# Matrix product with leaky ReLU by two levels of Strassen-Winograd: three more products in quarters, paired output transfers, and kept sums of B

## The chip, the cores and the metric

The kernel runs on one core of one Trainium2 chip. The core has five engines with queues of their own: PE (matmul), DVE (VectorE), ACT (ScalarE), POOL (GpSimd) and SP (SyncE, which here only issues DMAs). The metric is the device time of one execution in microseconds (us), as the median of several runs.

## The reference

```python
def setup_inputs():
    m, k, n = 4096, 4096, 4096
    return {"a": np.random.randn(m, k).astype(np.float32),
            "b": np.random.randn(k, n).astype(np.float32), "alpha": np.float32(0.01)}

def reference(a, b, alpha):
    x = np.matmul(a, b)
    return np.where(x > 0, x, alpha * x)
```

## The kernel before

A and B are rounded to 16-bit floats on the way in; the sums are kept in 32 bits. The output is cut into 4 groups of 1024 rows (g = 0 to 3) and 4 pairs of 1024 columns (j = 0 to 3). One such block (g, j) is a *region*; the first of all is done in the plain way, the other 15 stand in the list `regions` and are done one behind the other: j = 1, 2, 3 for g = 0, then 2, 0, 3, 1 for groups 1 and 2, and 2, 0, 1, 3 for group 3. Groups 2 and 3 are thus (2,2), (2,0), (2,3), (2,1), (3,2), (3,0), (3,1), (3,3).

**First level.** In a region A is a 2 x 2 of blocks a11 to a22, and B of b11 to b22 (a block is 512 x 2048 or 2048 x 512, in two halves k of 1024 along the inner dimension). Winograd's scheme needs seven products instead of eight, in the order of `PRODUCTS`: a11 b11, a12 b21, s2 T2, s3 T3, s1 T1, a22 T4, s4 b22. Here s1 to s4 are sums of blocks of A, made once in a group, and T1 to T4 are sums of blocks of B, made by DVE in place: T3 = b22 - b12 over b12, T2 = b11 + T3 over b11, and so on (`b_sum`, line 603). A whole product is 64 matmuls of 128 x 128 by 512 columns in the function `product` (line 831). It goes into four banks of PSUM, each 128 rows x 512 columns ("row tile" mt = 0 to 3). The eight banks are two sets, y and z, that change places with each region. After the first product ACT copies y to z (line 1132), so that the second product can be added on z while the third is added on y.

**Second level.** A product can be done in quarters: its operands are cut again into 2 x 2, and seven *quarter products* of 16 matmuls of 256 columns (`quarter_product`, line 770) take the place of eight. That needs four sums of the operand of A and four of that of B, of 128 x 2048 numbers each (`sums_of_a`, `sums_of_b`, lines 696 to 719 and 753; those of s1, s4, a22 are made once in a group, kept in DRAM and loaded as needed), and some copies and adds between banks. Before the change, groups 1 to 3 do the products of s3, s1, a22 and s4 in quarters; in most regions the order on PE is first, second, third product whole, then s1, s3, a22, s4 in quarters (`fifth_in_quarters`, `fourth_by_seeds`, `sixth_in_quarters`, `seventh_in_quarters`). The last region of a group ("turning") does most products whole, because ACT, DVE and POOL bring in the next group's A there.

**Order.** The order on each engine is written out by hand: every engine's queue holds its instructions in the order of the program. A buffer that is taken from a pool waits for the release of an earlier tile there. The 128 x 2048 buffers (`new_a16`, three of them), the tile `t` of four such (pool `x`) and the `c` tiles (32-bit results on their way out) matter here.

**Around the edge of two regions.** The seventh product of a region writes y, a bank `one` and a bank `other`; ACT copies (lines 999, 1003, 1008) and DVE adds (1005, 1009 from `other`, 1011 from y) collect it in the `c` tiles `kept_c`; then `leave` does the leaky ReLU on DVE (line 313) and SP issues the output (line 1076, one DMA for each row tile).

**Start of a region.** After the first product come the copies y to z, then T3 and T2 (line 603) out of b11, b12, b22. For j = 2, T3 and T2 are written to DRAM in group 1 and loaded in groups 2 and 3 in their place (`move_t`, line 529; T2 on ACT's queue, T3 as a part of `fetch_unit`). s2 is loaded in two halves (line 789), the second behind a DVE memset (line 788).

**Measures.** The kernel checks that the magnitudes of rows of A and columns of B are alike. For each block a *measure* squares four parts of 128 x 2048 on ACT (line 231) and adds them on DVE (lines 240 to 264). `EARLY` and `MEASURED` say in which region which block is measured: those of `EARLY` around the first product, the "middle" one of `MEASURED` around T3 and T2. At the end the last region decides from all (`judge`, lines 635 to 651), and a plain bf16 product would replace the result if they weren't alike.

Of the kernel before, what the change touches and what calls it, by code (L numbers as in the profile page):

```python
# [24 lines left out]
KC = 8  # L25
# [12 lines left out]
OTHERS = (0, 3)  # L38

# [9 lines left out]
def kernel(  # L49
# [464 lines left out]
    kept_t = {name: dram_pool.tile([2, P, KC * NT], DT, name=f"kept_{name}") for name in ("t3", "t2")}  # L514
# [12 lines left out]
    def move_t(name, t, k, out, queue=nc.sync):  # L527
        ends = kept_t[name][k], t.rearrange("p c n -> p (c n)")
        queue.dma_start(*(ends if out else ends[::-1]))

    def fetch_unit(i, u, nt, later=False):
# [7 lines left out]
        if g > 1 and j == CACHED and (half, nt) == (0, 1):  # L539
            move_t("t3", t, u, False)  # L540
# [89 lines left out]
    def judge(line):  # L630
# [29 lines left out]
        (1, 3): [B11], (2, 0): [B21], (2, 3): [B21], (2, 1): [B12], (3, 1): [B11, B21],  # L660
# [15 lines left out]
    FIFTH = {(1, 0), (1, 3), (2, 0), (2, 3), (3, 0), (3, 1), (3, 3)}  # L676
# [123 lines left out]
    in_quarters = False  # L800
    for i, (g, j) in enumerate(regions):
# [6 lines left out]
        ybank = 0 if i % 2 == 0 else 4  # L808
        zbank = 4 - ybank
# [6 lines left out]
        def product(n, banks, first):  # L816
            name, half, nt = PRODUCTS[n]

# [3 lines left out]
            if n == 0 or n == 2 and in_fourth:  # L822
                order[-16:] = [(mt, k, c) for mt in range(MT) for k, c in todo[-4:]]
            elif n == 1 or n == 4 and in_fourth:
                order[:16] = [(mt, k, c) for mt in range(MT) for k, c in todo[:4]]
# [14 lines left out]

        def keep(banks, side):
            pairs, kept = new_c(side)
            for mt in range(MT):
                nc.scalar.copy(kept[mt], banks[mt])  # L844
            return pairs, kept

# [51 lines left out]
        def fifth_in_quarters(y, banks, tq, sx, pairs, between):  # L898
# [6 lines left out]
            onto = lambda r, n: [y[2 * r + m][:, n * HALF:(n + 1) * HALF] for m in range(2)]  # L905
# [6 lines left out]
            def more(r, n, room):  # L912
                for m, to in enumerate(onto(r, n)):
                    nc.vector.tensor_add(to, to, room[:, m])

            quarter_product(x[0, 1], b[1, 0], onto(0, 0))
            quarter_product(x[0, 0], b[0, 0], into(chain), True)
            one = copied(0, 0, chain)
            quarter_product(a_quarter(sx[4]), b[1, 1], onto(0, 1))
# [3 lines left out]
            quarter_product(x[1, 1], t(4), onto(1, 0))  # L923
# [9 lines left out]
            last = copied(1, 1, chain)  # L933
            for m in range(2):
# [3 lines left out]
        def sixth_in_quarters(pairs, banks, v_pairs, v, y, tq, sq):  # L938
# [20 lines left out]
            add(v, y)  # L959
# [28 lines left out]
        def seventh_in_quarters(y, one, other, tq, sq):  # L988
# [7 lines left out]
            onto = lambda r, n: [y[2 * r + m][:, n * HALF:(n + 1) * HALF] for m in range(2)]  # L996
            quarter_product(x[0, 1], b[1, 0], onto(0, 0))
# [3 lines left out]
            quarter_product(x[1, 1], t(4), onto(1, 0))  # L1001
# [3 lines left out]
            nc.vector.tensor_add(block(0, 1), pair(other), block(0, 1))  # L1005
            quarter_product(sx(3), b[0, 1], into(one))
            for n in (1, 0):
                nc.scalar.copy(block(1, n), pair(one))
            nc.vector.tensor_add(block(1, 1), pair(other), block(1, 1))
            for mt in range(MT):  # L1010
                nc.vector.tensor_add(kept[mt], y[mt], kept[mt])
            return pairs

        def seventh_at_the_end(y, one, other, tq, sq, one_more):
# [9 lines left out]
            onto = lambda r, n: [part(y[2 * r + m], n) for m in range(2)]  # L1024
# [8 lines left out]
            for mt in (2, 3):  # L1033
                nc.scalar.copy(part(kept[mt], 1), part(y[mt], 1))
            quarter_product(x[0, 1], b[1, 0], onto(0, 0))
            for mt in range(2):
                more(mt, 0, part(y[mt], 0))
# [7 lines left out]
            quarter_product(sx(4), b[1, 1], onto(0, 1))  # L1045
            for mt in range(2):
                more(mt, 1, part(y[mt], 1))
# [7 lines left out]
            quarter_product(x[1, 1], t(4), onto(1, 0), by_row=True)  # L1055
            for mt in (2, 3):
                more(mt, 0, part(y[mt], 0))
# [12 lines left out]
        def leave(pairs, h, nt, some=(0, 1)):  # L1070
            for r, t in enumerate(pairs):
# [3 lines left out]
                for m in range(2):  # L1075
                    nc.sync.dma_start(place(g, h, 2 * r + m, j, nt), t[:, m, :])  # L1076
# [34 lines left out]
        y = [new_bank(ybank + mt) for mt in range(MT)]  # L1111
        z = [new_bank(zbank + mt) for mt in range(MT)]
# [6 lines left out]
        in_fifth = (g, j) in FIFTH  # L1119
        second_of_group = in_fourth and regions[i - 2][0] != g  # L1120
        early = [measure(i, *block) for block in EARLY.get((g, j), [])]
        for m in early[:1]:
# [3 lines left out]
        product(0, y, True)  # L1126
        if second_of_group:
            sums_of_s3(g, (2,))
        for m in early[:1]:
            m.end()  # L1130
        for mt in range(MT):
            nc.scalar.copy(z[mt], y[mt])  # L1132
        if second_of_group and g in [of for of, _ in FIFTH]:
            sums_of_a(g, "s1", new_a16)
        for m in early[1:]:
            m.begin()
# [19 lines left out]
        for m in early[1:]:  # L1156
# [43 lines left out]
        if in_fifth:  # L1200
# [8 lines left out]
        if in_fifth:  # L1209
# [6 lines left out]
        for k in ks:  # L1216
            halves_of = [slice(None)]
            if in_fifth and k == ks[1]:
# [7 lines left out]
            if in_fourth and k == ks[0]:  # L1226
                y7 = quarters_of_b(i, 0, 1)
                t3_of_b(y7)
                if not in_fifth:
                    tq = {n: new_a16() for n in (2, 1)}  # L1230
                    sums_of_b(y7, tq, (2, 1))
# [8 lines left out]
        z = [new_bank(zbank + mt) for mt in range(MT)]  # L1240
# [234 lines left out]
```

## Time and profile before

| | |
|---|---|
| median of 3 runs | 1524.78 us (1524.66 to 1526.13) |
| profiled execution, its own time | 1526.13 us |
| span from the first to the last instruction | 1524.2 us |
| mean granted clock of TensorE | 0.999 |
| DMA traffic | 372.29 MB, 244 GB/s on average |
| regions (2,0), (2,3), (3,0), (3,1), each from its start to the next region's | 90.34, 90.35, 90.34, 90.35 us |
| regions (1,0), (1,3) | 91.85, 91.90 us |
| turning regions (1,1), (2,1) | 95.11, 95.11 us |

How to read it: times in a row are us from the span's start. A row of the order in time has start, length, engine, line, operation, output and inputs, the count of merged instructions, and in brackets the idle time ahead with what ended it. A PE row's length goes to the modelled end of its last matmul, so rows overlap by some tenths; starts are compared. A row of waits has the waiting engine and line, what it waited for, then total, count and longest. A row of a stretch has its ends, its length, the busy time (and count) of PE, weight loads, DVE, ACT and POOL, then the granted clock, the DMA share and GB/s. "q" behind an engine's name is its queue of DMAs.

### The profile page before, as it was taken

The numbers are of one execution on the slowest core, as the hardware profiler recorded it, in microseconds if no ns is written. First come the engines' busy times: TensorE is split into PE (matmuls) and PEld (weight loads), VectorE is DVE, ScalarE is ACT, GpSimd is POOL, SyncE is SP. The second block draws the span as 40 slices with busy tenths as digits, with TensorE's granted clock in tenths as the row PEclk, the third lists the DMA queues.
The fourth block names the chain that finished last, engine by engine and source line by source line (L and its number), as shares of the span: only waits on it lengthen the run. The fifth ranks groups of instructions, "written<-read, shape, count | busy, mean of one in ns | idle before, by whom it ended". The sixth has DMA issues, their size and how long they took to land.

```text
span 1524.2 us, 22803 instructions
## 1 busy us (share of the span) xinstructions
PE 1512.9 (99%) x9003; PEld 879.2 (58%) x9003; DVE 1166.7 (77%) x1221; ACT 512.2 (34%) x885; POOL 258.3 (17%) x426
## 2 busy tenths in 40 slices
PE   9999999999999999999999999999999999999998
PEld 4444444444446577584544748667554475848667
DVE  4588867666896597777779598777978779888797
ACT  2411535537410123124661132323574113252221
POOL 5641110233202011012320101000331100101000
PEclk9999999999999999999999999999999999999999
DMA  9999995999889999999898968859999894968935
GB/s 247 189 215 206 242 285 164 174 187 193 235 330 247 285 300 288 290 289 271 199 273 317 287 252 187 312 151 330 220 239 313 223 337 148 276 238 205 331 122 172
DMA packets 197767, 372.29 MB, mean 244 GB/s; under 512 B 19345, under 2 KB 132241, under 8 KB 184594
## 3 DMA queue, kind: packets, MB, share of 16 engines
q0 software_dynamic: 119808, 112.22, 46.7%
q1 hardware_dynamic: 71218, 232.95, 41.0%
q10 hardware_dynamic: 6624, 25.56, 4.3%
q8 instruction: 72, 1.18, 0.3%
q14 instruction: 45, 0.37, 0.1%
HBM read 359.66 MB, written 121.11 MB: 315 GB/s over the span
## 4 chain that ended last, share of the span: by engine, by line
PE 58%; DMA 6%; DVE 1%; issue 1%; SPq 0%; POOL 0%; DVEq 0%; POOLq 0%
PE ps L831 34%; PE ps L770 25%; DMA b<-in_b_dram 5%; DMA q<-kept_qs 1%; DVE b L603 0%; DVE c L313 0%; DVE c L1028 0%; POOL b L547 0%; SPq L1076 0%; DVE b L696 0%; DVE b L1225 0%; SPq L762 0%; DVEq L603 0%; DVEq L313 0%; POOLq L547 0%
## 5 line engine op out<-in xcount | busy, mean ns | idle before, releaser
L831 PE MATMUL ps<-b,a 128*128 128x512 f16 x2624 | 570.6, 379 | 0.0
L831 PEld LDWEIGHTS <-a 128*128 128x128 f16 x2624 | 256.7, 98 | 307.8
L831 PE MATMUL ps<-b,s 128*128 128x512 f16 x1792 | 391.3, 379 | 0.0
L831 PEld LDWEIGHTS <-s 128*128 128x128 f16 x1792 | 175.4, 98 | 210.9
L603 DVE TENSOR_TENSOR b<-b 128x4096 f16<-128x4096 f16 x97 | 218.9, 2286 | 51.3 <-DMA b<-in_b_dram 33.1
L547 POOL DMA_DIRECT2D b<-in_b_dram x128 | 94.8, 745 | 870.5 <-PE ps L770 266.1
L770 PEld LDWEIGHTS <-q 128*128 128x128 f16 x1872 | 182.6, 98 | 23.2 <-DMA q<-kept_qs 1.6
L844 ACT COPY c<-ps 128x512 f32<-128x512 f32 x164 | 85.9, 596 | 287.5 <-PE ps L831 277.7
L133 POOL DMA_DIRECT2D a<-in_a_dram x252 | 137.5, 553 | 246.5 <-ACT junk L622 81.3
L142 DVE STREAM_TRANSPOSE a<-a 128x512 uint32<-128x512 uint32 (+2 forms) x120 | 127.0, 1107 | 66.5 <-DMA a<-in_a_dram 66.5
L313 DVE SCALAR_TENSOR_TENSOR c<-c 128x1024 f32<-128x1024 f32 (+2 forms) x123 | 141.9, 1196 | 17.7 <-ACT c L844 17.4
L622 ACT ACTIVATE junk<-a 128x512 bf16<-128x512 f16 x192 | 121.2, 631 | 72.8 <-DMA a<-in_a_dram 67.7
L770 PEld LDWEIGHTS <-a 128*128 128x128 f16 x1200 | 117.4, 98 | 14.7
L231 ACT ACTIVATE sq<-b 128x2048 bf16<-128x2048 f16 x60 | 111.3, 1911 | 43.1 <-DVE sq L240 36.7
L770 PE MATMUL ps<-b,q 128*128 128x256 f16 x1008 | 118.6, 273 | 0.0
L283 PE MATMUL ps<-b,a 128*128 128x512 f16 x512 | 112.2, 379 | 0.5 <-ACT a L380 0.2
L770 PEld LDWEIGHTS <-s 128*128 128x128 f16 x960 | 93.8, 98 | 14.2 <-DVE b L603 1.3
L770 PE MATMUL ps<-q,q 128*128 128x256 f16 x864 | 99.9, 273 | 0.9 <-DMA q<-kept_qs 0.9
L770 PE MATMUL ps<-b,a 128*128 128x256 f16 x752 | 88.3, 273 | 0.0
L283 PEld LDWEIGHTS <-a 128*128 128x128 f16 x512 | 49.7, 98 | 60.8 <-issue 1.4
L1132 ACT COPY ps<-ps 128x512 f32<-128x512 f32 x60 | 32.8, 572 | 147.8 <-PE ps L831 147.8
L1063 DVE TENSOR_TENSOR c<-ps,c 128x512 f32<-128x512 f32 x72 | 44.6, 683 | 47.6 <-PE ps L831 38.0
(125 smaller groups left out, 1053.6 us busy)
## 6 DMA issues: line engine op xcount, KB each, us to landing
b<-in_b_dram POOLq DMA_DIRECT2D x136, 512.0 KB, 12.4
out_dram<-c SPq DMA_DIRECT2D x240, 256.0 KB, 7.8
a<-in_a_dram POOLq DMA_DIRECT2D x244, 128.0 KB, 5.7
b<-kept_half SPq DMA_DIRECT2D x28, 1024.0 KB, 11.8
b<-kept SPq DMA_DIRECT2D x20, 1024.0 KB, 9.2
q<-kept_qs ACTq DMA_DIRECT2D x40, 512.0 KB, 7.2
s<-kept_s SPq DMA_DIRECT2D x18, 1024.0 KB, 9.1
q<-kept_qs SPq DMA_DIRECT2D x28, 512.0 KB, 6.1
```

The lines of the kernel that those rows point to most:

```text
L133: nc.gpsimd.dma_start(a16[32 * q:32 * q + 32], src.rearrange("(g i) w -> i g w", i=32))
L142: nc.vector.transpose(part.rearrange("p c m e -> p c (m e)").bitcast(U32) .rearrange("p c (g i) -> p g c i", i=32), src[:, :, i * n:(i + 1 ...
L231: nc.scalar.activation(to, self.parts[n], SQUARE)
L283: nc.tensor.matmul(ps, a_cols(at[0, h, u], c, mt, (h, u) == (0, 0)), bt[0, u, nt][:, c, :], start=first, stop=last,)
L313: nc.vector.scalar_tensor_tensor(t, t, alpha, t, op0=MULT, op1=MAX if alpha <= 1 else MIN)
L547: nc.gpsimd.dma_start(t[:, c:c + 4, :], b_rows(j, u, c, 4, nt, g > 0))
L603: nc.vector.tensor_tensor(f(to), f(x0), f(x1), op)
L622: nc.scalar.activation(junk, piece[:, q, :], SQUARE, accum_out=to[:, 4 * n + q:4 * n + q + 1])
L770: nc.tensor.matmul(to[m], xq[:, c // 2, rows, c % 2], yq[:, c, :], start=first and c == 0 and m < banks, stop=c == KC - 1, skip_group_chec ...
L831: nc.tensor.matmul(banks[mt], a_cols(t, c, mt, t is first_a), B(half, nt, k)[:, c, :], start=first and (k, c) == todo[0], stop=(k, c) == t ...
L844: nc.scalar.copy(kept[mt], banks[mt])
L1063: nc.vector.tensor_add(to, bank, to)
```

## The change

1. The first product (a11 b11) of (2,3), (3,1) and (3,3) is done in quarters (`first_in_quarters`). Its sums are made by DVE: seven in steps between the quarter products of the seventh product of the region before (`for_the_first`), the eighth in the first product. The four banks of y then hold quarters instead of row tiles, so the second and third product of these regions are cut into matmuls of 256 columns, and all helpers that read y or z go by quarters there. s2 is loaded behind the first product in these regions.
2. `leave` issues one DMA for two row tiles.
3. T3 and T2 are also kept for j = 0 and 3: written in group 2, loaded in group 3.
4. Measures: B21 of j = 0 goes from (2,0) to (3,0), B11 of j = 1 from (3,1) to (1,1). In a region whose first product is in quarters, or which loads T2, the early measures come behind the copies to z; where T2 is loaded, such a measure is begun and ended at once.
5. The set `FIFTH` (all regions in question had their fifth product in quarters) and the branches for the others go.

```diff
+KEPT_T = {CACHED: 1, 0: 2, 3: 2}
...
+    def places(g, h, mt, j, nt):
+        row = ((g * 2 + h) * MT + mt) * P
+        col = (j * 2 + nt) * NT
+        return out[row:row + 2 * P, col:col + NT].rearrange("(m p) n -> p m n", p=P)
...
-        if g > 1 and j == CACHED and (half, nt) == (0, 1):
-            move_t("t3", t, u, False)
+        if g > KEPT_T.get(j, G) and (half, nt) == (0, 1):
+            move_t("t3", j, t, u, False)
...
     EARLY = {
-        (1, 3): [B11], (2, 0): [B21], (2, 3): [B21], (2, 1): [B12], (3, 1): [B11, B21],
+        (1, 3): [B11], (1, 1): [B11], (2, 3): [B21], (2, 1): [B12], (3, 0): [B21], (3, 1): [B21],
     }
...
+    FIRST = {(2, 3), (3, 1), (3, 3)}
...
+        in_first = (g, j) in FIRST
+        if in_first:
+            shared_bank = Z[1]
+            Y, Z = [Z[2], Z[3], Y[0], Z[0]], [Y[1], Y[2], Z[1], Y[3]]
+        else:
+            Y, Z = Z, Y
...
+            if in_first:
+                for k in ks:
+                    for q in (0, 1, 3, 2):
+                        for c in range(KC):
+                            for m, to in enumerate(into(banks[q])):
+                                nc.tensor.matmul(
+                                    to, a_cols(operand(g, name, k), c, q // 2 * 2 + m),
+                                    B(half, nt, k)[:, c, q % 2 * HALF:(q % 2 + 1) * HALF],
+                                    start=False, stop=(k, c) == (ks[-1], KC - 1), skip_group_check=True,
+                                )
+                return
...
-        def seventh_in_quarters(y, one, other, tq, sq):
+        def seventh_in_quarters(y, one, other, tq, sq, between):
...
+            quarter_product(x[0, 1], b[1, 0], onto(y, 0, 0))
             quarter_product(x[0, 0], b[0, 0], into(one), True)
             nc.scalar.copy(block(0, 0), pair(one))
-            quarter_product(sx(4), b[1, 1], onto(0, 1))
-            quarter_product(x[1, 1], t(4), onto(1, 0))
+            quarter_product(sx(4), b[1, 1], onto(y, 0, 1))
+            next(between)
+            quarter_product(x[1, 1], t(4), onto(y, 1, 0))
+            next(between)
             quarter_product(sx(2), t(2), into(one))
             nc.scalar.copy(block(0, 1), pair(one))
+            next(between)
             quarter_product(sx(1), t(1), into(other), True)
+            next(between)
             nc.vector.tensor_add(block(0, 1), pair(other), block(0, 1))
             quarter_product(sx(3), b[0, 1], into(one))
+            next(between)
             for n in (1, 0):
                 nc.scalar.copy(block(1, n), pair(one))
             nc.vector.tensor_add(block(1, 1), pair(other), block(1, 1))
-            for mt in range(MT):
-                nc.vector.tensor_add(kept[mt], y[mt], kept[mt])
+            add_pieces(pairs, y)
             return pairs
+
+        def for_the_first(tq, sq, first_t, first_s):
+            y1 = quarters_of_b(i + 1, 0, 0)
+            x1 = {key: by_chunk(q) for key, q in quarters_of_a(g, "a11").items()}
+            tt = nc.vector.tensor_tensor
+            f = lambda n: b_quarter(first_t[n])
+            fx = lambda n: by_chunk(first_s[n])
+            first_s[1] = new_a16()
+            tt(fx(1), x1[1, 0], x1[1, 1], ADD)
+            yield
+            first_s[2] = tq[4]
+            tt(fx(2), fx(1), x1[0, 0], SUB)
+            yield
+            first_t[3], first_t[2] = new_a16(), tq[2]
+            tt(f(3), y1[1, 1], y1[0, 1], SUB)
+            tt(f(2), f(3), y1[0, 0], ADD)
+            yield
+            first_t[1], first_s[3] = new_a16(), tq[1]
+            tt(f(1), y1[1, 1], f(2), SUB)
+            tt(fx(3), x1[0, 0], x1[1, 0], SUB)
+            yield
+            first_s[4] = sq[3]
+            tt(fx(4), x1[0, 1], fx(2), SUB)
+            yield
+
+        def first_in_quarters(y, shared, z, tq, sq):
+            room = new_c(side)[0][1][:, :, :HALF]
+            b = quarters_of_b(i, 0, 0)
+            x = quarters_of_a(g, "a11")
+            one, other, third, chain = y
+            t = lambda n: b_quarter(tq[n])
+            sx = lambda n: a_quarter(sq[n])
+            quarter_product(x[0, 0], b[0, 0], into(chain), True)
+            nc.scalar.copy(one, chain)
+            quarter_product(sx(1), t(1), into(shared), True)
+            nc.scalar.copy(room, pair(shared))
+            tq[4] = new_a16()
+            nc.vector.tensor_tensor(t(4), b[1, 0], t(2), SUB)
+            quarter_product(sx(2), t(2), into(chain))
+            nc.scalar.copy(other, chain)
+            quarter_product(x[0, 1], b[1, 0], into(one))
+            nc.scalar.copy(z[0], one)
+            quarter_product(sx(3), t(3), into(chain))
+            nc.scalar.copy(third, chain)
+            nc.vector.tensor_add(pair(chain), pair(chain), room)
+            quarter_product(sx(4), b[1, 1], into(other))
+            nc.vector.tensor_add(pair(other), pair(other), room)
+            quarter_product(x[1, 1], t(4), into(third))
+            z[2] = new_bank(Z[2])
+            for to, bank in ((3, chain), (1, other), (2, third)):
+                nc.scalar.copy(z[to], bank)
...
-                for m in range(2):
-                    nc.sync.dma_start(place(g, h, 2 * r + m, j, nt), t[:, m, :])
+                nc.sync.dma_start(places(g, h, 2 * r, j, nt), t)
...
+        have_t2 = g > KEPT_T.get(j, G)
+        at_once, afterwards = ([], early) if in_first or have_t2 else (early[:1], early[1:])
+        for m in at_once:
             m.begin()
...
+        if in_first:
+            shared = new_bank(shared_bank)
+            first_in_quarters(y, shared, z, first_t, first_s)
+            new_s(g, "s2")
+            load_s2(g, ks[0])
+        else:
+            product(0, y, True)
...
-        have_t2 = g > 1 and j == CACHED
         if have_t2:
             for k in ks:
                 t = have_b[i, k, 0] = b_pool.tile([P, KC, NT], DT, name="b", tag="b11")
-                move_t("t2", t, k, False, nc.scalar)
+                move_t("t2", j, t, k, False, nc.scalar)
+        for m in afterwards:
+            m.begin()
+            if have_t2:
+                m.end()
         if middle:
             middle.begin()
         for k in ks:
             if have_t2:
+                if late_s2:
+                    load_s2(g, ks[1], True)
                 break
             b_sum(B(0, 1, k), B(1, 1, k), B(0, 1, k), SUB)
...
             b_sum(B(0, 0, k), B(0, 1, k), B(0, 0, k), ADD)
-            if g == 1 and j == CACHED:
-                move_t("t3", B(0, 1, k), k, True)
-                move_t("t2", B(0, 0, k), k, True)
+            if g == KEPT_T.get(j):
+                move_t("t3", j, B(0, 1, k), k, True)
+                move_t("t2", j, B(0, 0, k), k, True)
         if middle:
             middle.end()
-        for m in early[1:]:
+        for m in [] if have_t2 else afterwards:
             m.end()
...
-                kept_c = seventh_in_quarters(*rest)
+                first_t, first_s = {}, {}
+                between = for_the_first(tq, sq, first_t, first_s) if next_first else nothing()
+                kept_c = seventh_in_quarters(*rest, between)
                 fetch_b(i + 1, [(1, 1)], (1, 0))
-                new_s(g, "s2")
-                load_s2(g, 1)
+                if not next_first:
+                    new_s(g, "s2")
+                    load_s2(g, 1)
                 leave(kept_c, 0, 1)
```

More of the change, by code (lines that the diff above doesn't have):

```diff
@@ L525, in fetch_b, with move_t @@
                 fetch_unit(i, 2 * half + k, nt)
-    def move_t(name, t, k, out, queue=nc.sync):
-        ends = kept_t[name][k], t.rearrange("p c n -> p (c n)")
+    def move_t(name, j, t, k, out, queue=nc.sync):
+        ends = kept_t[name, j][k], t.rearrange("p c n -> p (c n)")
         queue.dma_start(*(ends if out else ends[::-1]))
@@ L800 @@
     in_quarters = False
+    Y, Z = [4, 5, 6, 7], [0, 1, 2, 3]
     for i, (g, j) in enumerate(regions):
@@ L839, in new_c, with onto, pieces, add_pieces @@
             return pairs, [pairs[mt // 2][:, mt % 2, :] for mt in range(MT)]
+        def onto(y, r, n):
+            if in_first:
+                return into(y[2 * r + n])
+            return [y[2 * r + m][:, n * HALF:(n + 1) * HALF] for m in range(2)]
+        def pieces(pairs, banks):
+            if in_first:
+                return [(pairs[q // 2][:, :, q % 2 * HALF:(q % 2 + 1) * HALF], pair(banks[q])) for q in range(4)]
+            return [(pairs[mt // 2][:, mt % 2, :], banks[mt]) for mt in range(MT)]
         def keep(banks, side):
             pairs, kept = new_c(side)
-            for mt in range(MT):
-                nc.scalar.copy(kept[mt], banks[mt])
+            for to, bank in pieces(pairs, banks):
+                nc.scalar.copy(to, bank)
             return pairs, kept
+        def add_pieces(pairs, banks):
+            for to, bank in pieces(pairs, banks):
+                nc.vector.tensor_add(to, bank, to)
         def fourth_in_quarters(banks, tq, sx):
@@ L1238 @@
             keep_x21(g, "a22")
-        z = [new_bank(zbank + mt) for mt in range(MT)]
+        z = [new_bank(Z[mt]) for mt in range(MT)]
         def s3_fourth(room):
```

142 lines of the change are left out of this document (66 added, 76 removed).

## The prediction

> **What bounds the kernel now.** I read the page first, then the waits of PE, then PE, DVE, ACT and SP in order of time around the edges of the regions.
>
> ```profile
> PE 1512.9 (99%) x9003; PEld 879.2 (58%) x9003; DVE 1166.7 (77%) x1221; ACT 512.2 (34%) x885; POOL 258.3 (17%) x426
> ...
> PE ps L770 <- DMA q<-kept_qs: 0.9, 1, 0.9
> PE ps L770 <- DVE b L1225: 0.6, 2, 0.3
> ...
> PE ps L770 <- DVE b L603: 0.6, 1, 0.6
> ```
>
> PE is the bound: behind the start it waits four times, all in the two middle regions of group 1, and never in groups 2 and 3, where the change works. So a gain needs fewer PE cycles, and any new wait is paid in full. The price of a product comes from starts on PE (times and lengths in us):
>
> ```profile
> 942.48 1.91 PE L770 MATMUL ps<-b,a 128*128 128x256 f16 x16
> ...
> 954.71 3.66 PE L770 MATMUL ps<-b,s 128*128 128x256 f16 x32
> ...
> 959.95 1.91 PE L770 MATMUL ps<-q,s 128*128 128x256 f16 x16
> 961.69 3.66 PE L770 MATMUL ps<-q,q 128*128 128x256 f16 x32
> 965.19 1.91 PE L770 MATMUL ps<-b,q 128*128 128x256 f16 x16
> 966.93 27.79 PE L831 MATMUL ps<-b,a 128*128 128x512 f16 x128
> 994.56 13.98 PE L831 MATMUL ps<-b,s 128*128 128x512 f16 x64
> 1008.37 3.66 PE L770 MATMUL ps<-b,s 128*128 128x256 f16 x32
> ```
>
> A product in quarters takes 954.71 - 942.48 = 12.23 us (112 matmuls at 0.1092; one quarter product of 16 takes 1.75), a whole one 1008.37 - 994.56 = 13.81 us (64 at 0.2158).
>
> **The change part by part.** *PE work.* Three first products go from 13.81 to 12.23: -1.58 each. In these regions the second and third products are cut into 128 matmuls of 256 columns, 128 x 0.1092 = 13.98 instead of 13.81, +0.17 twice. Net -1.25 per region, -3.75 in all if nothing waits.
>
> *The edge.* Seven sums of 128x2048 now stand in DVE's queue inside the seventh product before each such region, an eighth in the first product. Before, DVE did this there (and the next row gives the pitch of such sums, 1.14, or 1.26 if one needs the last):
>
> ```profile
> 965.44 0.69 DVE L1005 TENSOR_TENSOR c<-ps,c 128x512 f32<-128x512 f32 x1 [5.74 <-issue]
> 967.75 0.69 DVE L1009 TENSOR_TENSOR c<-ps,c 128x512 f32<-128x512 f32 x1 [1.61 <-ACT c L1008]
> ...
> 921.88 1.23 DVE L702 TENSOR_TENSOR q<-b 128x2048 f16<-128x2048 f16 x1
> 923.14 1.23 DVE L704 TENSOR_TENSOR q<-b,q 128x2048 f16<-128x2048 f16 x1
> 924.28 1.22 DVE L706 TENSOR_TENSOR q<-b,q 128x2048 f16<-128x2048 f16 x1
> ...
> 944.48 0.57 ACT L958 COPY ps<-ps 128x512 f32<-128x512 f32 x1 [1.16 <-PE ps L770]
> ```
>
> The 5.74 + 1.61 us idle seem to be cover for 7 x 1.14 = 8.0. But each sum is written where an operand of the running product lay, so it waits for its quarter product: fx1 for the third (ends 959.95), fx2 for the fourth, f3 for the fifth (963.44). DVE starts 0.25 behind PE's end (965.19 to 965.44), so f3 starts at 963.69, f2 at 964.95, f1 at 966.21, fx3 at 967.35, the L1005 add at 968.49, fx4 at 969.1 and the L1009 add at 970.24 instead of 967.75, done at 970.93. L1009 is the last reader of the bank into which the new first product copies its first quarter (`one` is the seventh's `other`). That ACT copy takes 0.57 (the L958 row): 970.97 to 971.54. The third quarter product of the new first accumulates on the source of that copy; it could start at 966.93 + 2 x 1.75 = 970.43 and starts at about 971.6. **Stall 1.2 us per edge**, 3.6 in all: of 3.75 about 0.15 remains. On ACT the copy of the second quarter product is queued behind, to a `c` buffer whose earlier contents must have left:
>
> ```profile
> 963.39 0.33 SPq L1076 DMA_DIRECT2D out_dram<-c  x1
> ...
> out_dram<-c SPq DMA_DIRECT2D x1, 256.0 KB, 10.1
> ```
>
> That transfer landed at 973.5, 6.6 behind the edge; the copy and the next one then end at about 7.8, just ahead of the fifth quarter product (at 6.99 plus the 1.2 of the stall). If the copy of the first quarter were not late, this one would cost 0.8 instead. So the bounds of an edge are 0.8 and, with a landing 1.7 later still, 2.5 (an estimate). I take 1.2.
>
> *The rest of these regions.* The leaky pass of kept_c ends some 2.3 later than before, then come the eighth sum and two adds, the last behind the sixth quarter product (6 x 1.75 + 1.2 + 0.25, and 0.7 long: 12.7); in (2,3) and (3,1) T3 and T2 (four of 2.27) and the measure of B21 (7.1, from L240 to the end, rows below) follow, then leaky (2.3) and three sums of 2.27: 12.7 + 9.1 + 7.1 + 2.3 + 6.8, so L696 starts 38.0 behind the region's start. What that may be, two regions show: in (1,0) L696 started 546.24 - 504.21 = 42.03 behind the start, in (3,0) 1286.32 - 1245.91 = 40.41.
>
> ```profile
> 546.24 1.22 DVE L696 TENSOR_TENSOR b<-b 128x2048 f16<-128x2048 f16 x1
> ...
> 504.21:596.06 91.85, 90.94 (x643) 62.39 (x641) 70.09 (x70) 16.79 (x30) 11.84 (x16) 1.00 1.06 293
> ...
> 1245.91:1336.25 90.34, 90.34 (x642) 62.55 (x640) 76.18 (x80) 24.11 (x34) 5.92 (x8) 1.00 0.80 241
> ```
>
> The labels of the last two rows are the regions' starts and ends. (1,0) took 91.85, (3,0) (its L696 is quoted below) 90.34 with PE busy throughout: 1.51 lost. So **L696 may start up to 40.5 behind a region's start, and each us beyond costs one**. 38.0 is free.
>
> *T3 and T2 kept.*
>
> ```profile
> L603 DVE TENSOR_TENSOR b<-b 128x4096 f16<-128x4096 f16 x97 | 218.9, 2286 | 51.3 <-DMA b<-in_b_dram 33.1
> ...
> b<-kept_t ACTq DMA_DIRECT2D x4, 1024.0 KB, 10.5
> ```
>
> In (2,0) and (2,3) four writes of 1 MB each are issued on SP behind the sums, some 10 us ahead of the next loads that PE needs: 0. In (3,0) and (3,3) four sums of 2.27 = 9.1 us of DVE fall away and T2 is loaded through ACT's queue behind the copies that follow the first product. It lands in 10.5 and the third product reads it 12.5 after its issue: free, with 2 us to spare. The T3 load takes the place of one on POOL's queue.
>
> *The measures.* B21 leaves (2,0), where nothing waited: gain 0. B11 goes to (1,1), where DVE sat idle 5.72 at that place, and nothing on PE waited for it: 0. But B21 now stands in **(3,0), right ahead of the measure of B22**, which was there already. Before (the first row is that of (1,1)):
>
> ```profile
> 699.85 2.29 DVE L603 TENSOR_TENSOR b<-b 128x4096 f16<-128x4096 f16 x1 [5.72 <-DMA b<-kept_half]
> ...
> 1259.70 1.06 ACT L1132 COPY ps<-ps 128x512 f32<-128x512 f32 x2 [2.39 <-PE ps L831]
> 1261.35 5.51 ACT L231 ACTIVATE sq<-b 128x2048 bf16<-128x2048 f16 x3 [0.59 <-DVE q L719]
> 1271.60 1.91 ACT L231 ACTIVATE sq<-b 128x2048 bf16<-128x2048 f16 x1 [4.74 <-DVE sq L240]
> ...
> 1270.35 1.22 DVE L240 TENSOR_TENSOR sq<-sq 128x2048 bf16<-128x2048 bf16 x1
> 1273.54 1.23 DVE L243 TENSOR_TENSOR sq<-sq 128x2048 bf16<-128x2048 bf16 x1 [0.65 <-ACT sq L231]
> 1277.45 2.35 DVE L313 SCALAR_TENSOR_TENSOR c<-c 128x1024 f32<-128x1024 f32 x2
> 1286.32 1.22 DVE L696 TENSOR_TENSOR b<-b 128x2048 f16<-128x2048 f16 x1
> ```
>
> A measure is three squares on ACT (5.5), a fourth (1.9), the L243 add and its fold to the end, 1277.45 - 1273.54 = 3.9 on DVE (from L240 on, 7.1). In the new order ACT issues the two T2 loads from 1260.8, squares B21 from about 1261.6 (B22 started at 1261.35 before) to 1269.0, and DVE ends it at 1273.0. B22's first square needs a buffer that L243 of B21 frees, at 1270.3; its four squares end at 1277.75 and DVE at 1281.7. DVE no longer makes T3 and T2 in that time, but it only waits for ACT. Behind the measure stand, in DVE's queue as before, leaky and three sums (1286.32 - 1277.45 = 8.9): L696 starts at 1290.6, 44.7 behind the region's start. **PE waits 44.7 - 40.5 = 4.2 us.** The least, with buffers free at once: 8 squares x 1.84 from 1261.6 and 3.9 behind, 1280.2, gives 2.7; with the buffers freed in the worse order, 5.5. In (3,3), counted from its start, ACT squares B22 from 15.2, DVE ends the measure at 26.6, leaky waits for the second product's copies (to 30.1), two sums end at 34.6, the decision takes 3.1 and a third sum 2.3:
>
> ```profile
> 1461.57 0.59 DVE L644 TENSOR_REDUCE most<-line 1x2 f32<-1x256 f32 x1
> ...
> 1464.67 2.27 DVE L603 TENSOR_TENSOR b<-b 128x4096 f16<-128x4096 f16 x1
> ```
>
> L696 comes at 40.0: free, by half a us.
>
> *Output in pairs.* 240 DMAs become 120 of double size and the same bytes. It may help at one place, the load (L762) for which PE waits 0.9 in (1,3):
>
> ```profile
> 631.49 0.66 SPq L1076
> ...
> 632.20 0.71 SPq L762
> ```
>
> One issue fewer (0.66) stands ahead of it, but the bytes are the same. Gain 0 to 0.7; I take 0.3.
>
> **Sum**: -3.75 + 3.6 + 4.2 - 0.3 = +3.75. The profiled run took 1526.13 (span 1524.2 and 1.9 around), 1.35 above the median; 1526.13 + 3.75 = 1529.9, and against the median 1524.78 + 3.75 = **1528.5 us**.
>
> **The rivals.**
> *A, (3,0) does not wait*: the T3 and T2 sums removed give back what the second measure takes. For it: 9.1 us of DVE against 7.1. Against it: ACT's 8 squares cannot start before 1261.6, whatever DVE does. It holds if L696 of (3,0) starts by 40.5; then -0.45, 1524.3: not slower.
> *B, the edges do not wait*, (3,0) does: the copy would have to be free of L1009, and the `c` buffer to land by 5. -3.75 + 4.2 - 0.3 = +0.15, 1524.9.
> *C, neither waits*: -4.05, 1520.7.
> *D, transfers come late as well*: the `c` buffer at the edges at 2.5 each (+3.9 over the sum) or T2 later than its 2 us: about 1532.
> *E, the clock falls in the gap of (3,0).* After the last matmuls the granted clock (third number from the end of a row) went:
>
> ```profile
> 1515.31 1.91 PE L770 MATMUL ps<-q,s 128*128 128x256 f16 x16
> ...
> 1520.00:1521.00 1.00, 0.00 (x0) 0.00 (x0) 0.00 (x0) 0.00 (x0) 0.00 (x0) 1.00 0.57 211
> ...
> 1522.00:1524.00 2.00, 0.00 (x0) 0.00 (x0) 0.00 (x0) 0.00 (x0) 0.00 (x0) 0.50 0.01 5
> ```
>
> It held for about 4 us of idleness (1517.2 to 1521); the gap in (3,0) is 3.5 in one piece, then 0.5. If it fell and took as long to come back, half of 4 us is lost: +2, 1530.5. The Trainium skill ("TensorE: Matmul & The Clock Gate", "What's actually happening") says that the clock is halved after at least one idle window of about 3.4 us, and comes back after a busy one; by that the sum would be 1.7 higher, 1530.2, if a whole free-running window fell into the gap. The trace agrees in kind with its 4 us.
>
> **How the numbers follow.** The forecast has 0.57, A 0.10, B 0.10, C 0.14, D 0.06, E 0.03. The forecast's own range is 1526.3 to 1531 (2.7 to 5.5 in (3,0), 0.8 to 1.6 at an edge). The range 1522.8 to 1532 takes in A, B, E and part of D and leaves out C and the rest of D. 0.2% is 3.05 us, about what a measurement of this kernel tells from no change: slower beyond 1527.8 is 0.7 of the forecast, D and E, 0.49; within is the rest of the forecast, A and B, 0.37; faster is C, 0.14.
>
> **What would show it.** A wait of the copy in `first_in_quarters` for DVE at all three edges, and a PE start about 1.2 late in each first product; first products that take 13.4 rather than 12.2. In (3,0), two runs of four squares on ACT, L696 44 to 45 behind the region's start, and PE waiting for DVE's b sums about 4 us. Wrong it is if (3,0) lasts 90.3 as before, or if the regions (2,3), (3,1), (3,3) are over 1 us shorter than before.

## The result, and the profile after

| | before | after |
|---|---|---|
| median of 6 runs each | 1524.79 us (1524.66 to 1526.13) | 1535.6 us (1529.54 to 1538.57) |
| profiled execution, its span | 1526.13, 1524.2 us | 1538.57, 1536.7 us |
| mean granted clock | 0.999 | 0.997 |
| regions (2,0), (2,3), (3,0), (3,1) | 90.34, 90.35, 90.34, 90.35 us | 90.35, 90.27, 101.61, 90.27 us |

The changed kernel takes 1.0065 times as long (95% interval 1.0046 to 1.0084), 10.8 us more. The prediction had the sign and put 1528.5 us. The profiled execution is the longest of the six.

The busy row of the page:

```profile
PE 1513.6 (98%) x9531; PEld 932.1 (61%) x9531; DVE 1179.9 (77%) x1231; ACT 519.1 (34%) x897; POOL 252.2 (16%) x418
```

The waits of PE (what waited, for what: total, times, longest):

```profile
PE ps L777 <- DVE b L610: 5.1, 2, 3.8
PE ps L854 <- DMA s<-kept_s: 3.7, 1, 3.7
PE ps L777 <- ACT ps L1101: 3.1, 3, 1.0
```

Before, PE waited 2.0 us in all behind the start, and never in groups 2 and 3. Now three lines are new or larger: three waits of 1.0 for the copy at the edges, one of 3.7 for s2, one of 3.8 for the sums of b. The stretches, (1,0), (1,3), (2,0), (2,3), (3,0), (3,1) in this order, show where they lie:

```profile
505.82:598.40 92.58, 90.84 (x643) 62.50 (x641) 70.09 (x70) 16.78 (x30) 11.84 (x16) 1.00 1.04 290
598.40:689.42 91.02, 90.76 (x643) 62.46 (x641) 69.27 (x74) 24.10 (x34) 7.40 (x10) 1.00 1.07 290
878.04:968.39 90.35, 90.35 (x642) 62.57 (x640) 75.01 (x74) 16.80 (x30) 5.92 (x8) 1.00 0.91 290
968.39:1058.66 90.27, 89.24 (x818) 79.79 (x816) 74.74 (x77) 26.46 (x38) 5.91 (x8) 1.00 0.93 287
1247.29:1348.90 101.61, 94.04 (x643) 63.75 (x641) 78.38 (x90) 31.39 (x38) 5.92 (x8) 0.97 0.78 235
1348.90:1439.17 90.27, 89.24 (x819) 79.79 (x816) 79.66 (x81) 26.38 (x38) 2.98 (x4) 1.00 0.77 260
```

(2,3) and (3,1) have 1.1 us less PE work (89.24 against 90.35 busy) and are 0.08 shorter: what the first product in quarters saves, the edge takes. (3,0) is 11.27 longer, and it is the one region whose mean clock is under 1.00. All the loss in groups 2 and 3 is there.

The edge from (2,0) to (2,3), in order of time, first PE, then DVE, then ACT:

```profile
968.39 1.91 PE L777 MATMUL ps<-b,a 128*128 128x256 f16 x16
970.14 1.91 PE L777 MATMUL ps<-q,q 128*128 128x256 f16 x16
973.08 1.91 PE L777 MATMUL ps<-q 128*128 128x256 f16 x16 [1.03 <-ACT ps L1101]
...
965.10 1.23 DVE L1080 TENSOR_TENSOR q<-b 128x2048 f16<-128x2048 f16 x1 [0.52 <-PE ps L777]
...
970.55 1.22 DVE L1088 TENSOR_TENSOR q<-a,q 128x2048 f16<-128x2048 f16 x1
971.68 0.69 DVE L1057 TENSOR_TENSOR c<-ps,c 128x512 f32<-128x512 f32 x1
...
972.46 0.57 ACT L1101 COPY ps<-ps 128x512 f32<-128x512 f32 x1 [2.79 <-DVE c L1057]
973.55 0.58 ACT L1103 COPY c<-ps 128x512 f32<-128x512 f32 x1 [0.53 <-DMA out_dram<-c]
```

The third quarter product was due at 970.14 + 1.75 = 971.89 and starts at 973.08, 1.19 late. The add (L1057) stands behind five sums and ends at 972.37; the copy starts 0.1 later, and PE 0.05 behind the copy's end. The copy behind it (L1103) waits for its output transfer, but is still in time for the fifth quarter product.

In (3,0), first PE, then ACT with its DMA queue, DVE, and SP's queue:

```profile
1247.29 27.79 PE L854 MATMUL ps<-b,a 128*128 128x512 f16 x128
1274.91 7.07 PE L854 MATMUL ps<-b,s 128*128 128x512 f16 x32
1285.73 8.75 PE L854 MATMUL ps<-b,s 128*128 128x512 f16 x32 [3.75 <-DMA s<-kept_s]
1298.31 5.34 PE L777 MATMUL ps<-b,s 128*128 128x256 f16 x32 [3.83 <-DVE b L610]
1303.48 1.91 PE L777 MATMUL ps<-b,q 128*128 128x256 f16 x16
...
1261.38 0.33 ACTq L536 DMA_DIRECT2D b<-kept_t  x1
...
1262.55 3.71 ACT L237 ACTIVATE sq<-b 128x2048 bf16<-128x2048 f16 x2 [0.40 <-DVE q L726]
1273.05 3.71 ACT L237 ACTIVATE sq<-b 128x2048 bf16<-128x2048 f16 x2 [6.79 <-DMA kept_qs<-q]
1278.05 7.31 ACT L237 ACTIVATE sq<-b 128x2048 bf16<-128x2048 f16 x4 [1.29 <-DVE sq L249]
...
1280.74 0.06 DVE L795 MEMSET s<- 128x1 f16 x1
...
1298.17 1.22 DVE L703 TENSOR_TENSOR b<-b 128x2048 f16<-128x2048 f16 x1
...
1255.75 7.11 SPq L727 DMA_DIRECT2D kept_qs<-q  x4
1280.84 0.32 SPq L796 DMA_DIRECT2D s<-kept_s  x1
```

Four things are to be seen. The eight squares of the two measures do stand behind each other, as forecast. But the third square waits 6.79 us for the write of a sum of s1 to DRAM, because it takes over the buffer that this write reads; before, three squares ran without a break there. The sums of b (L703) therefore start 1298.17 - 1247.29 = 50.9 behind the region's start, not 44.7. And the second half of s2 is loaded only at 1280.84, since the memset ahead of it (L795) stands in DVE's queue behind the first measure; PE waits for it.

The clock, in stretches around these two gaps of PE (clock: third number from the end):

```profile
1281.00:1285.70 4.70, 0.98 (x5) 0.25 (x4) 2.76 (x3) 4.70 (x4) 0.00 (x0) 1.00 0.62 223
1285.80:1289.20 3.40, 3.40 (x9) 1.19 (x9) 3.23 (x7) 1.49 (x4) 0.00 (x0) 0.50 0.01 2
1289.20:1294.00 4.80, 4.80 (x24) 2.17 (x23) 4.80 (x7) 1.52 (x3) 0.00 (x0) 1.00 0.55 200
...
1299.40:1302.80 3.40, 3.40 (x19) 2.39 (x18) 3.37 (x3) 0.00 (x0) 0.00 (x0) 0.51 0.37 149
```

Behind each gap the clock is 0.50 or 0.51 for 3.4 us. Behind the second one 32 matmuls of 256 columns take 1303.48 - 1298.31 = 5.17 us instead of 3.49, 1.68 lost.

**What sets the loss of (3,0).** Without any wait the first product in quarters (s1 T1, from L777 on) would start behind three whole ones, 27.62 + 13.81 = 41.43 behind the region's start, at 1288.72. It starts at 1298.31, 9.59 late, as soon as the last of the L610 sums, which stand ahead of L703 in DVE's queue, is done; the slow clock behind that adds 1.68: 11.27, the whole. The wait for s2 and the slow clock behind it lie inside the 9.59: had they not been, PE would have waited as much longer for the sums of b.

### The profile page after: what moved, and what is told of

Read it like the earlier page. It is cut to its first block, busy times and chain, and to the rows that moved or that the text cites. A ratio compares the mean times of both kernels' runs of the same rounds, so it can differ in the third digit from the quotient of the medians.

```text
span 1536.7 us, 23690 instructions
## 1 busy us (share of the span) xinstructions
PE 1513.6 (98%) x9531; PEld 932.1 (61%) x9531; DVE 1179.9 (77%) x1231; ACT 519.1 (34%) x897; POOL 252.2 (16%) x418
## 3 DMA queue, kind: packets, MB, share of 16 engines
q8 instruction: 76, 1.25, 0.3%
## 5 line engine op out<-in xcount | busy, mean ns | idle before, releaser
L854 PE MATMUL ps<-b,a 128*128 128x512 f16 x2240 | 487.2, 379 | 0.0
L854 PEld LDWEIGHTS <-a 128*128 128x128 f16 x2240 | 219.2, 98 | 263.0
L854 PE MATMUL ps<-b,s 128*128 128x512 f16 x1600 | 351.3, 380 | 3.7 <-DMA s<-kept_s 3.7
L854 PEld LDWEIGHTS <-s 128*128 128x128 f16 x1600 | 156.9, 98 | 193.6 <-DVE sq L248 4.2
L610 DVE TENSOR_TENSOR b<-b 128x4096 f16<-128x4096 f16 x89 | 200.8, 2287 | 39.4 <-DMA b<-in_b_dram 32.5
L777 PEld LDWEIGHTS <-q 128*128 128x128 f16 x2064 | 201.5, 98 | 27.9 <-issue 4.0
L777 PEld LDWEIGHTS <-a 128*128 128x128 f16 x1344 | 131.5, 98 | 16.3
L777 PE MATMUL ps<-b,q 128*128 128x256 f16 x1056 | 124.3, 273 | 0.0
L289 PE MATMUL ps<-b,a 128*128 128x512 f16 x512 | 112.5, 379 | 1.5 <-DVE a L143 0.9
L777 PE MATMUL ps<-q,q 128*128 128x256 f16 x960 | 111.3, 273 | 0.1
L777 PEld LDWEIGHTS <-s 128*128 128x128 f16 x960 | 94.6, 99 | 19.2 <-DVE b L610 6.3
L777 PE MATMUL ps<-b,a 128*128 128x256 f16 x848 | 99.8, 273 | 0.0
L289 PEld LDWEIGHTS <-a 128*128 128x128 f16 x512 | 49.6, 98 | 62.3 <-issue 1.9
L1246 ACT COPY ps<-ps 128x512 f32<-128x512 f32 x48 | 26.4, 572 | 129.8 <-PE ps L854 129.8
L777 PE MATMUL ps<-b,s 128*128 128x256 f16 x544 | 64.2, 277 | 5.7 <-DVE b L610 5.1
```

The costliest lines, as they stand in the source:

```text
L289: nc.tensor.matmul(ps, a_cols(at[0, h, u], c, mt, (h, u) == (0, 0)), bt[0, u, nt][:, c, :], start=first, stop=last,)
L610: nc.vector.tensor_tensor(f(to), f(x0), f(x1), op)
L777: nc.tensor.matmul(to[m], xq[:, c // 2, rows, c % 2], yq[:, c, :], start=first and c == 0 and m < banks, stop=c == KC - 1, skip_group_chec ...
L854: nc.tensor.matmul(banks[mt], a_cols(t, c, mt, t is first_a), B(half, nt, k)[:, c, :], start=first and (k, c) == todo[0], stop=(k, c) == t ...
```

## The experiments

Theory: the loss is made by DVE's sums coming late in (3,0), through the two measures, the late write under the third square, and the clock behind the gap; the first products gain nothing because of the edge stall. Rivals: the s2 load is a cost of its own; the output pairs or the `c` buffers cost; the first products in quarters are slower for another reason. "Before" is the kernel before on the same chip, beside each run: medians 1526.8 us in the first group, 1525.37 in the second, 1524.19 in the third.

**1. B21 of j = 0 measured in (2,0) again** (all else as changed).

```diff
-        (1, 3): [B11], (1, 1): [B11], (2, 3): [B21], (2, 1): [B12], (3, 0): [B21], (3, 1): [B21],
+        (1, 3): [B11], (1, 1): [B11], (2, 0): [B21], (2, 3): [B21], (2, 1): [B12], (3, 1): [B21],
```

> The changed kernel with the measure of B21 of j = 0 back in (2,0). Theory 1 (the loss is the two measures in a row in (3,0), with what waits behind them): (3,0) goes from 101.6 us back to 90.3, the median to 1524.3 to 1525, and the spread of the runs shrinks to that of the kernel before (about 1.5). Rival (the kept T3 and T2, their transfers and the edges cost it): (3,0) or other regions stay long, median above 1528.

Measured: 1526.18 us, ratio 0.9997 (0.9988 to 1.0006). One edit takes back the whole loss. Its stretch of (3,0), and in it the square and the sum:

```profile
1245.61:1337.11 91.50, 90.85 (x643) 62.47 (x641) 72.10 (x80) 24.09 (x34) 5.91 (x8) 1.00 0.85 260
```

```profile
1270.76 3.71 ACT L237 ACTIVATE sq<-b 128x2048 bf16<-128x2048 f16 x2 [6.41 <-DMA kept_qs<-q]
...
1287.29 1.22 DVE L703 TENSOR_TENSOR b<-b 128x2048 f16<-128x2048 f16 x1
```

The third square still waits 6.41 us for the write, but with one measure alone that nearly fits: L703 comes 41.68 behind the start, and (3,0) is 1.16 longer than before (it was expected to be no longer); the prediction's rule (one us for each us beyond 40.5) gives 1.18. The three edge waits of 1.03 are unchanged.

**2. s2's second half loaded ahead of the measures** (B21 in (3,0)).

```diff
                 move_t("t2", j, t, k, False, nc.scalar)
+            if late_s2:
+                load_s2(g, ks[1], True)
         for m in afterwards:
...
             if have_t2:
-                if late_s2:
-                    load_s2(g, ks[1], True)
                 break
```

> The changed kernel with the load of the second half of s2 ahead of the measures in (3,0) and (3,3). Theory 1a (two waits in (3,0), one for s2 behind the measure of B21, 3.9 us, one for the sums of b behind both measures, 4.0, and after each the clock at half for 3.4 us, 1.7 each): the wait for s2 goes, with the clock drop behind it, PE reaches the end of the third product 5.6 earlier and so waits for b, which comes no sooner, up to 9.5 in one piece, with one drop of the clock: 1.7 less, about 1534. Rival (the wait for s2 is the root): 1528 or less.

Measured: 1534.91 us (1531.11 to 1537.56), ratio 1.0053 (1.004 to 1.0066). The wait for s2 is gone, and no gain can be told: (3,0) takes 99.67, with one gap in place of two. That is 1.9 less than in the first profile of the changed kernel, but no less than in its three later ones (99.42 to 100.11, run 9), and the medians, 1534.91 and 1535.6, lie well within the spread of either kernel's runs. The third product and the first quarter products behind it on PE, and the stretch after:

```profile
1273.15 13.98 PE L854 MATMUL ps<-b,s 128*128 128x512 f16 x64
1293.54 6.42 PE L777 MATMUL ps<-b,s 128*128 128x256 f16 x32 [6.41 <-DVE b L610]
```

```profile
1293.50:1296.90 3.40, 3.36 (x16) 2.41 (x17) 3.39 (x3) 0.00 (x0) 0.00 (x0) 0.50 0.57 230
```

The rival that s2 costs by itself falls: it was a wait ahead of a later wait on the same engine.

**3. T2 loaded behind the first three squares of B21** instead of ahead of them.

```diff
-        if have_t2:
+        if have_t2 and not afterwards:
             for k in ks:
                 t = have_b[i, k, 0] = b_pool.tile([P, KC, NT], DT, name="b", tag="b11")
                 move_t("t2", j, t, k, False, nc.scalar)
         for m in afterwards:
             m.begin()
             if have_t2:
+                for k in ks:
+                    t = have_b[i, k, 0] = b_pool.tile([P, KC, NT], DT, name="b", tag="b11")
+                    move_t("t2", j, t, k, False, nc.scalar)
                 m.end()
```

> The changed kernel with the loads of T2 in (3,0) behind the first three squares of B21 on ACT's queue. Theory 1b (the third square waits 6.8 us for the buffer of a sum of s1 whose write to DRAM shares the queues with T2's 2 MB): that square starts by 1267 instead of 1273, counted as in the changed kernel's profile, the measure of B21 ends 6 us earlier and b's sums come at 44 to 45 behind the region's start; T2, issued 5 later, may cost a new wait of 1 to 3 on PE; median 1527 to 1533. Rival (the write is slow by itself): the square still starts at about 1273 and nothing gets shorter.

Measured: 1529.35 us, ratio 1.0017 (1.0008 to 1.0026), with both measures in (3,0). This is the case that the prediction had in mind. ACT with its queue, and PE:

```profile
1260.24 3.72 ACT L237 ACTIVATE sq<-b 128x2048 bf16<-128x2048 f16 x2
1263.02 0.81 ACTq L536 DMA_DIRECT2D b<-kept_t  x2
1263.85 3.70 ACT L237 ACTIVATE sq<-b 128x2048 bf16<-128x2048 f16 x2
...
1289.11 1.92 PE L777 MATMUL ps<-b,s 128*128 128x256 f16 x16 [2.02 <-DVE b L610]
```

The four squares run with no wait, T2 still comes in time, (3,0) lasts 93.31 (2.97 over before) and its clock is 1.00 throughout. So the write was held by the T2 load. The time from issue to landing of the four writes (least, median, most), in the changed kernel and then in this one:

```profile
DMA to landing us min/median/max: 5.4/5.4/10.4
```

```profile
DMA to landing us min/median/max: 2.6/4.9/4.9
```

The last write, issued at 1262.5 in the changed kernel, lands at 1272.9. The second T2 load, issued at 1261.83 and taking 11.0, lands at 1272.8. With T2 issued behind it the last write takes 2.6. In the changed kernel the two queues moved this in the 4.0 us from 1262.5 on, and then until both had landed (q10 is ACT's queue with the load, q1 is SP's with the write; packets, MB, share of the 16 DMA engines):

```profile
q10 hardware_dynamic: 156, 1.16, 80.0%
q1 hardware_dynamic: 9, 0.03, 1.8%
...
q10 hardware_dynamic: 119, 0.84, 35.5%
q1 hardware_dynamic: 143, 0.52, 19.6%
```

So the bytes of the write were late themselves: its 512 KB moved only in the second stretch, when more than half of the load had gone ahead of them. Why the load went first no run shows. The Trainium skill ("DMA: Bandwidth & Descriptors", "Queues, rings and completion order") says that the write which signals a DMA's end lands only after all earlier writes of the same DMA engine, across its queues. The two landings at the same time are in keeping with that, but with the bytes late already, no run here shows what that rule adds.

**4. The output in pairs alone**, on the kernel before.

```diff
-                for m in range(2):
-                    nc.sync.dma_start(place(g, h, 2 * r + m, j, nt), t[:, m, :])
+                nc.sync.dma_start(places(g, h, 2 * r, j, nt), t)
```

> The kernel before with the output in pairs of row tiles alone. Theory: 0 to -0.7 us, from the load in (1,3); 1524.1 to 1524.8. Rival (512 KB transfers hold the queues longer, seen as the longer wait in (1,0) of the changed kernel, 1.30 instead of 0.56): slower by 0.5 to 1.

Measured: 1525.43 us, ratio 0.9997 (0.9988 to 1.0005): nothing that can be told.

**5. No first product in quarters**, with the edit of 1: `FIRST = set()`.

> The changed kernel with B21 of j = 0 back in (2,0) and no first product in quarters. Theory 2 (a wait of 1.19 at each edge takes back all but 0.08 of what a first product in quarters saves): within 0.5 of the kernel with B21 back alone, ratio to the kernel before 0.9995 to 1.001. Rival (the edges gain a us or more each): slower than that kernel by 3.

Measured: 1524.51 us, ratio 0.9991 (0.9982 to 1.0). Without them the kernel is not slower than run 1 with them (0.9997): as changed, they gain nothing. (The ratio is a little under the 0.9995 that was expected as the least, and its interval takes that in.)

**6. fx3 and fx4 made behind the add that the copy waits for**, with the edit of 1.

```diff
-            first_t[1], first_s[3] = new_a16(), tq[1]
+            first_t[1] = new_a16()
             tt(f(1), y1[1, 1], f(2), SUB)
-            tt(fx(3), x1[0, 0], x1[1, 0], SUB)
             yield
-            first_s[4] = sq[3]
+            first_s[3], first_s[4] = tq[1], sq[3]
+            tt(fx(3), x1[0, 0], x1[1, 0], SUB)
...
             quarter_product(sx(3), b[0, 1], into(one))
-            next(between)
             for n in (1, 0):
                 nc.scalar.copy(block(1, n), pair(one))
             nc.vector.tensor_add(block(1, 1), pair(other), block(1, 1))
+            next(between)
```

> B21 back in (2,0), and of the seven sums at an edge the two for the third and fourth sum of a11 behind the last adds of `other`. Theory 2: the copy that PE waits for comes 2 us earlier; what is left of the wait is that for the c buffer, 0 to 0.9 per edge at the fifth quarter product; 1 to 3.5 us less than with B21 back alone, ratio to before 0.9975 to 0.999. Rival (the wait is for another reader of the bank, or for PE's own start): no change.

Measured: 1522.22 us, ratio 0.9979 (0.997 to 0.9988), 2.3 us under run 5 of the same group. The edge, ACT and then PE:

```profile
969.24 0.57 ACT L1101 COPY ps<-ps 128x512 f32<-128x512 f32 x1 [0.67 <-PE ps L777]
972.84 0.59 ACT L1103 COPY c<-ps 128x512 f32<-128x512 f32 x1 [3.04 <-DMA out_dram<-c]
973.32 0.59 ACT L1107 COPY ps<-ps 128x512 f32<-128x512 f32 x1
...
970.78 1.91 PE L777 MATMUL ps<-q 128*128 128x256 f16 x16
...
974.27 1.91 PE L777 MATMUL ps<-q,q 128*128 128x256 f16 x16
```

The copy (L1101) now waits for PE alone, and the third quarter product starts at 970.78, on time. The copy to the `c` buffer waits 3.04 us for the output; the copy behind it ends at 973.91, and the fifth quarter product needs it at 974.27: 0.36 to spare. (2,3) lasts from 967.29 to 1056.37, 89.08: 1.27 less than before.

**7. The same, and the copy to the `c` buffer moved behind the next copy**, so that nothing waits for the output transfer there.

```diff
-            nc.scalar.copy(room, pair(shared))
             tq[4] = new_a16()
...
             nc.scalar.copy(other, chain)
+            nc.scalar.copy(room, pair(shared))
```

> As the run with the adds first, and on ACT the copy into the c buffer behind the copy of the next quarter product. Theory 2: no wait of PE at the three edges, 3.6 less than with B21 back alone; ratio to before 0.997 to 0.998. Rival (the c buffer lands early enough anyway): the same as with the adds first.

Measured: 1522.17 us, ratio 0.9978 (0.9969 to 0.9988): as run 6. The output transfer is no bound at the edge, against the 0.8 us that the prediction gave as its least.

**8. The best of all: run 7, and T3 and T2 kept for j = 3 only** (`KEPT_T = {CACHED: 1, 3: 2}`).

> As the run before, and T3 and T2 of j = 0 not kept, so that (3,0) makes them as the kernel before did. Theory 1b: with T2 loaded in (3,0) the write of a sum of s1 still held back the third square of B22 by 6.4 us and cost 1.16 on PE; without it (3,0) takes 90.35, 1.2 less than the run before; ratio to before 0.996 to 0.9975. Rival (the sums of T3 and T2 on DVE cost as much): no change.

Measured: 1521.93 us (1521.3 to 1523.15), ratio 0.9977 (0.9968 to 0.9987). It beats both kernels, by 0.23% the one before, and no wait of PE is left in groups 2 and 3; but from runs 6 and 7 it can't be told apart. The 1.2 us expected here were not there to be won: (3,0) lasts 90.42, and in the profile of run 7, with T2 loaded, it already lasted 90.35; the held write landed in 8.1 us there, against 10.2 in run 1. Keeping T3 and T2 for j = 0 showed neither a gain nor a loss once B21 is back in (2,0).

**9. The changed kernel three times more**, to see what varies.

> The changed kernel unaltered, profiled once more, to see which of the losses in (3,0) vary from one execution to the next. In its first profile (3,0) took 101.6 us: 3.75 waiting for s2, 3.83 for the b sums, and 1.68 for each of two falls of the granted clock; the rest of the span was near that of before. Theory (late writes of the fourth sum of s1, and the memset of s2 queued behind the measure, then the clock): the three edges again show 1.03 of waiting each and (3,1), (2,3) 90.3; the wait of the third square of B22 and with it both waits in (3,0) differ, and the whole time follows them, each gap over 3.4 us with 1.7 more. Rival (the spread is elsewhere, in group 1 or at the start): (3,0) again takes 101 to 102 whatever the time.

> As the run before, a second execution: time between 1529.5 and 1538.6; its distance from the first profile (1538.6) lies in (3,0) by the theory, to within 1.5 us, and elsewhere by the rival.

> As the two runs before, a third execution, with the same expectations.

Measured: 1534.64, 1534.3 and 1534.05 us, with (3,0) at 100.11, 99.60 and 99.42. In the third of them, PE and ACT:

```profile
1280.89 7.07 PE L854 MATMUL ps<-b,s 128*128 128x512 f16 x32 [1.39 <-DMA s<-kept_s]
1293.56 5.42 PE L777 MATMUL ps<-b,s 128*128 128x256 f16 x32 [5.61 <-DVE b L610]
1298.82 1.91 PE L777 MATMUL ps<-b,q 128*128 128x256 f16 x16
...
1268.30 3.71 ACT L237 ACTIVATE sq<-b 128x2048 bf16<-128x2048 f16 x2 [4.59 <-DMA kept_qs<-q]
```

The third square waited 4.40, 4.12 and 4.59 us here and 6.79 in the first profile. The wait for s2 moves with it (1.3 to 1.5 against 3.75), and is too short for the clock to fall; behind the gap of 5.6 it falls. This is called the usual case below, since three of the four profiled executions of this kernel show it. The 3.9 to 4.5 us to the first profile lie in (3,0) for 1.5 to 2.2; the rest was lost ahead of it, against the theory: (1,0) began 1.4 to 1.6 later there, in the plain first part of the kernel, and lasted 0.6 to 0.9 longer.

## Why the prediction was right in sign and wrong in size

**PE work: right.** -1.25 per region was forecast; with the edge free (run 6) it is -1.27.

**The edge: right.** 1.2 forecast, 1.19 measured, by the chain that was named: L1057 late behind the sums, the copy late behind it. Run 6 shows it by taking that chain away. The bound of 0.8 from the `c` buffer was too pessimistic: in run 6 the buffer came 5.5 behind the edge, not 6.6, with transfers in pairs. So rival B's edge can be had, but by another order of the sums; as changed it did not hold.

**The rest of these regions: right.** The sums of b were forecast 38.0, 38.0 and 40.0 behind the starts of (2,3), (3,1) and (3,3), and came at 37.6, 37.6 and 39.6; nothing on PE waited for them.

**The output in pairs: no effect**, 0.3 forecast; below what can be measured.

**(3,0): wrong in size.** The place, the engine and the rule were right, and rivals A and C fell. The loss was put at 4.2, 5.5 at worst. It was 9.1 to 11.3. The step that failed is the one that had T2's load "free, with 2 us to spare" and ACT squaring B21 "from about 1261.6 to 1269.0" in a row. For T2's own reader it was free: it landed at 1272.8 and PE started the third product at 1274.91, so rival D's late T2 isn't what happened. But the load is issued 0.7 us ahead of the last write of s1's sums on another queue, that write then lands with the load, and the third square needs the buffer under it. By run 3 without this the two measures cost 2.97 (L703 43.5 behind the start, not 44.7; the least forecast was 2.7). In the usual case L703 goes from 43.5 to 48.6, 5.1 more, of which the wait for the write is 4.6; the clock adds 1.77, less the 0.77 that PE otherwise waits in the quarter products behind the first: 2.97 + 5.1 + 1.77 - 0.77 = 9.1, the measured 99.42 - 90.34. In the first profile L703 moves by 7.4 (6.8 of it the write) and the clock adds 1.68: 11.3.

**The clock (rival E): underrated.** It was priced at 1.7 to 2.0 and given 0.03, since a gap of 3.5 us seemed barely enough. Once the gap was longer, it fell each time. The Trainium skill's rule of an idle window of about 3.4 us ("TensorE: Matmul & The Clock Gate", "What's actually happening") agrees: gaps of 3.75, 3.83, 5.6 and 6.41 us halved the clock, those of 1.39 and 2.02 did not. The 4 us of idleness through which the clock held at the end of the kernel before were thus no least length for a fall.

**Not seen: the memset of s2** behind the measure in DVE's queue. It made a wait of 1.3 to 3.75 us, but cost nothing beside the later one (run 2).

**Against the whole**: 3 x -0.08 and 9.1 make +8.9; measured are +9.9 to +10.5 in the three last runs beside a single 1524.19, and +10.8 in the medians. The remaining 1 to 2 us are within what the kernel before varies (1523.57 to 1528.9 in the runs beside the experiments). What makes the time of the changed kernel vary by 9 us from run to run is settled in part only: the late write and the clock in (3,0), and the first part of the kernel, where the cause stays open.

## What to carry to other kernels

A load that is "free" for its own reader can still be paid for by a small transfer issued just behind it: list what is issued in its shadow, and which buffers those transfers release. When work is moved in front of a queue that already ends just in time (here 40.4 of 40.5 us), every later surprise on that queue is paid in full, so such a place wants a margin and not a balance. When two waits of one engine follow each other, only the one that ends last is worth an edit.

## What the runs showed of the hardware that was not expected

A write of 0.5 MB whose like landed in 2.6 us took 7.8 to 10.4 when two loads of 1 MB were issued on another engine's queue just ahead of it; in the changed kernel its bytes moved only when more than half of the load's had. Gaps of PE of 3.75 us and more were followed by 3.4 us and more at half the clock, 1.7 us lost each time and up to 2.8 (run 2: 32 matmuls of 256 columns in 6.25 us instead of 3.49; the clock was 0.50 in the first 3.4 us and still 0.66 on average in the next, with PE busy throughout).
